# Hybrid RG-LRU, RWKV-7 and mLSTM layer: the state products, the inverse and the scores of two heads as one 128-wide product

## The chip, the cores and the metric

The kernel runs on one core of one Trainium2 chip, alone. The metric is the device time of one launch in microseconds. The kernel before was run three times, and one more execution was profiled; all rows below come from that one.

## What is computed

One layer of a streaming encoder in fp32, on a prompt of 2048 frames and a sample of 32 frames that continues other streams. The cut reference:

```python
hn = rmsnorm(x, norm1)
proj = hn @ w_in                                  # 1024 -> 3072 columns
ya = rmsnorm(rg_lru(causal_conv(pa_x)), norm_a) * gelu(pa_g)      # 256 channels
yb = rwkv7_mix(pb, state)                         # 6 heads x 64
yc = mlstm_mix(pc, state)                         # 6 heads x 64
x = x + concat(ya, yb, yc) @ w_out
gu = rmsnorm(x, norm2) @ w_ffn_in
x = x + (silu(gu[:, :D_FF]) * gu[:, D_FF:]) @ w_ffn_out           # D_FF = 2816
y = rmsnorm(x, norm_f)

# RWKV-7, one frame, per head (64 x 64 state S):
S = S * w_t[None, :] - (S @ kk_t)[:, None] * kka_t[None, :] + v_t[:, None] * k_t[None, :]
y_t = S @ r_t

# mLSTM, one chunk of 64 frames, per head:
scores = (q @ k.T) * exp(log_w - m)
num = w_inter * (q @ C0) + scores @ v
```

All states are outputs too.

## The kernel before

**Layout.** Channels lie on the partitions, frames along the rows. A tile of 128 channels holds two heads of 64, so the six heads of RWKV or mLSTM are three tiles of two, numbered `p` (0 to 2) and `j` (the half, 0 or 1). The prompt is handled in 4 superblocks of 512 frames; the last takes the sample's 32 frames along. The big products (`proj`, tiles `pj` in PSUM) split each fp32 operand into two parts of a shorter format and add three products: `ah,wh`, `al,wh`, `ah,wl`, or `hh`, `hl` for the FFN's hidden values. `phase2` is the output projection, the FFN and the final norm of one superblock. It loads the mixers' outputs from memory (`sq<-ymix`, tile k of 128 channels; k = 0, 1 are RG-LRU, 2 to 4 RWKV, 5 to 7 mLSTM), and `x<-x,pj` evicts into the residual, whose squares `acc` sums for the norm.

**Mixers.** They work in blocks of 128 frames, two chunks of 64, 16 blocks for the prompt and one of 32 frames (one chunk, padded) for the sample: 33 chunks in 17 blocks. `group` records `rwkv`, `mlstm` and `rglru` of one block after another. Their PSUM tiles are called `rw` and `ml`.

RWKV turns the recurrence of a chunk into products. `Fr` holds the scaled keys and receptances of a chunk, with zeros in the other head's half; `SV` holds the state (upper or lower 64 partitions by head) above V. The triangular system of a chunk is inverted in 32x32 blocks: `Hr` goes to memory (`tb`) and back (`xs<-tb`), VectorE does 31 steps of forward substitution (`utmp<-Z,xs`, `Z<-Z,utmp`), Z goes to memory and back (`c<-zb`, the tile `c`, called Zf in the code), and two small products of 32x32 (`ta,Hr` and `c,En`) give the block below the diagonal, where `ta` is the transposed diagonal block (called XT) that VectorE writes. Then per chunk: `xps` = Fr x SV, its copy X1 (tile `zc`), `ups` = Zf x X1, its copy `UV` (with a minus), `sps` = Fr x UV, which is added into the state S; with the state before the chunk, `Un` and `Hr` give the outputs, `hmE` starts their normalisation over the head, `h60E` to `h62E` are its small steps, `yx` is the result, which is transposed by three products with the identity (`cst,yx`), put through E and stored to `ymix`. An fp32 product on TensorE leaves two records in the trace. mLSTM multiplies q and k of a chunk into `sc` (`ml<-q,xi`), weighs the result (`Dm`) into `QS`, and updates its state R.

**Order.** All operations are first recorded with the tiles that they read and write, and `Recorder.order` then lays out every engine's queue by list scheduling, with the planner's own durations (`cost`; an fp32 product that is 64 wide counts 92 ns, one that is 128 wide 217). Mixer operations (priority 1) come ahead of the projections' (2) on TensorE, which fill what is left. A debt counter lets mixer products gather into bursts:

```python
hold = debt > (BURST if burst else 0.0)
...
debt = max(debt, 0.0) + o.dur
...
debt -= o.dur * RATE        # a projection product; RATE = 0.45
```

The queues are then issued in this order; nothing is reordered on the chip. `fill(phase2, ...)` of superblock i is recorded behind the mixers of superblock i, so it fills while the mixers of superblock i + 1 run. The third one, over frames 1024 to 1535, is the last that has mixers beside it; the fourth (544 columns in two pieces of 272) needs all of them.

Of the kernel before, what the change touches and what calls it, by code (L numbers as in the profile page):

```python
# [11 lines left out]
F32 = mybir.dt.float32  # L12
# [32 lines left out]
for _name, _w in (  # L45
    ("ident", 128), ("mar", 128), ("tri", 128), ("blk2", 2), ("mmask", 64), ("smask", 384), ("cmrow", 128),
    ("one", 1), ("sel", 384), ("bones", 128),
):
    CST[_name] = (_n, _w)
    _n += _w  # L50
# [16 lines left out]
def make_consts():  # L67
# [22 lines left out]
    put("smask", np.tile(np.where(t64 == 0, 0.0, 1.0), 6)[None])  # L90
    put("cmrow", np.tile(np.where(t64 == 0, NEG, 0.0), 2)[None])
# [330 lines left out]
def hybrid_kernel(ctx, tc, A, O, cfg):  # L422
# [81 lines left out]
    def setup():  # L504
# [36 lines left out]
        for wn, o in (("wq", 0), ("wk", 36)):  # L541
# [3 lines left out]
            wt = rws.tile([128, 3, 128], F32, tag="c" if o else "ta", name="wt")  # L545
# [269 lines left out]
    def rglru(src, n, st, col):  # L815
        def rt(nm):
            return mls.tile([128, 2, n], F32, tag={"xa": "xi", "r0": "q", "r1": "k", "r2": "Dm", "r3": "WI", "r4": "wl"}[nm], name=nm)
# [84 lines left out]
    def rwkv(src, n_real, nch, st, col):  # L902
# [21 lines left out]
        c_, ta = t3("c"), t3("ta")  # L924
# [20 lines left out]
        V.tensor_tensor_scan(out=cf, data0=C("smask", 0, 3 * n), data1=c_.rearrange("p a t -> p (a t)"), initial=0.0, op0=ALU.mult, op1=ALU.add)  # L945
# [90 lines left out]
        Zf = rw([128, 6, 64], "c")[:, :nq]  # L1036
        for b in range(4):
            h = 32 * (b % 2)
            SY.dma_start(Zf[32 * b:32 * b + 32, :, h:h + 32],
                         zb[:, 32 * nq * b:32 * nq * (b + 1)].rearrange("i (q e) -> i q e", e=32))  # L1040
            if h:
                G.memset(Zf[32 * b:32 * b + 32, :, 0:32], 0.0)
# [24 lines left out]
        V.transpose(out=XT, in_=Zf[:, :, 0:32])  # L1067
# [12 lines left out]
        for q in range(nq):  # L1080
            for j in range(2):
                t, b = slice(64 * j, 64 * j + 32), slice(64 * j + 32, 64 * j + 64)
                PE.matmul(po[t, q, :], NT[b, q, :], Zf[b, q, 32:64], start=True, stop=True,
                          tile_position=(64 * j + 32, 64 * j))
        for j in range(2):
            t = slice(64 * j, 64 * j + 32)
            S.activation(Zf[t, :, 32:64], po[t], AF.Copy, scale=-1.0)
# [550 lines left out]
```

## Time and profile before

| | us |
|---|---|
| three runs | 2846.54, 2850.44, 2855.05 |
| median | 2850.44 |
| profiled execution, own time | 2846.7 |
| its span in the trace | 2844.9 |
| TensorE busy in it | 2749.6 (97%) |
| VectorE busy in it | 2146.1 (75%) |
| mean granted TensorE clock | 0.987 of full speed |

The time contains 1.8 us more than the span from first to last instruction. Busy TensorE time contains matmuls whose ends are modelled and overlap; a product's price is therefore read from the starts of its neighbours. All engine instructions of the kernel share line 332 (the recorder's emit), so the rows are told apart by the tiles' names.

### The profile page before, as it was taken

The numbers are of one execution on the slowest core, as the hardware profiler recorded it, in microseconds if no ns is written. First come the engines' busy times: TensorE is split into PE (matmuls) and PEld (weight loads), VectorE is DVE, ScalarE is ACT, GpSimd is POOL, SyncE is SP. The second block draws the span as 40 slices with busy tenths as digits, with TensorE's granted clock in tenths as the row PEclk, the third lists the DMA queues.
The fourth block names the chain that finished last, engine by engine and source line by source line (L and its number), as shares of the span: only waits on it lengthen the run. The fifth ranks groups of instructions, "written<-read, shape, count | busy, mean of one in ns | idle before, by whom it ended". The sixth has DMA issues, their size and how long they took to land. (4 is left out here: it accounts for less than half of the span.)

```text
span 2844.9 us, 48298 instructions
## 1 busy us (share of the span) xinstructions
PE 2749.6 (97%) x17609; PEld 2310.6 (81%) x17609; DVE 2146.1 (75%) x6009; ACT 1281.1 (45%) x2830; POOL 43.7 (2%) x170
## 2 busy tenths in 40 slices
PE   9999999999999999999999999999999999999998
PEld 7877777889777777777777777777787778999997
DVE  6778877877887878789878888888676676554555
ACT  5555554655553444455444444454433334322223
POOL 0000000000000000000000000000000000000000
PEclk9999999999999999999999999999999999999999
DMA  7453534444323333335233333353332235232232
GB/s 238 133 168 116 179 105 143 138 132 121 121 72 108 88 100 99 95 112 160 73 108 98 89 96 94 100 162 78 100 109 83 84 89 161 81 89 87 88 93 77
DMA packets 235210, 317.92 MB, mean 112 GB/s; under 512 B 63100, under 2 KB 146988, under 8 KB 234844
## 3 DMA queue, kind: packets, MB, share of 16 engines
q1 hardware_dynamic: 233820, 313.72, 37.3%
q8 instruction: 138, 2.26, 0.3%
q10 hardware_dynamic: 1152, 1.11, 0.1%
q14 instruction: 100, 0.82, 0.1%
HBM read 268.50 MB, written 46.27 MB: 111 GB/s over the span
## 5 line engine op out<-in xcount | busy, mean ns | idle before, releaser
L332 PE MATMUL pj<-ah,wh 128*128 128x512 f32 (+1 forms) x2560 | 898.7, 359 | 3.2 <-ACT wh L332 1.1
L332 PE MATMUL pj<-al,wh 128*128 128x512 f32 (+1 forms) x2560 | 898.9, 358 | 2.5 <-DVE al L332 2.5
L332 PE MATMUL pj<-ah,wl 128*128 128x512 f32 (+1 forms) x2560 | 828.8, 356 | 1.5 <-DVE wl L332 1.5
L332 ACT ACTIVATE wh<-raw 128x1024 fp32r<-128x1024 f32 (+2 forms) x444 | 382.3, 861 | 728.8 <-PE pj L332 604.8
L332 PEld LDWEIGHTS pj<-ah,wh 128*128 128x128 f32 x2560 | 484.5, 190 | 68.7 <-ACT ah L332 1.6
L332 PEld LDWEIGHTS pj<-al,wh 128*128 128x128 f32 x2560 | 486.7, 190 | 63.9 <-DVE al L332 3.4
L332 PEld LDWEIGHTS pj<-ah,wl 128*128 128x128 f32 x2560 | 454.9, 189 | 66.8 <-DVE wl L332 3.1
L332 DVE TENSOR_TENSOR wl<-raw,wh 128x1024 fp32r<-128x1024 f32 (+2 forms) x444 | 433.0, 976 | 62.1 <-ACT wh L332 56.4
L332 PE MATMUL pj<-hh,wh 128*128 128x512 f32 (+1 forms) x856 | 299.6, 360 | 9.4 <-ACT hh L332 9.2
L332 PE MATMUL pj<-hl,wh 128*128 128x512 f32 (+1 forms) x856 | 300.9, 359 | 0.1
L332 PE MATMUL pj<-hh,wl 128*128 128x512 f32 (+1 forms) x856 | 280.9, 357 | 0.0
L332 DVE TENSOR_TENSOR x<-x,pj 128x512 f32<-128x512 f32 (+1 forms) x280 | 159.2, 584 | 126.4 <-PE pj L332 122.3
L332 PEld LDWEIGHTS pj<-hh,wh 128*128 128x128 f32 x856 | 160.9, 189 | 35.1 <-ACT hh L332 13.8
L332 PEld LDWEIGHTS pj<-hl,wh 128*128 128x128 f32 x856 | 162.3, 190 | 22.6 <-DVE hl L332 1.7
L332 PE MATMUL pj<-ah,hh 128*128 128x512 f32 (+1 forms) x480 | 170.1, 361 | 6.6 <-ACT hh L332 5.8
L332 PEld LDWEIGHTS pj<-hh,wl 128*128 128x128 f32 x856 | 152.8, 189 | 22.2
L332 PE MATMUL pj<-al,hh 128*128 128x512 f32 (+1 forms) x480 | 169.6, 360 | 0.0
L332 PE MATMUL pj<-ah,hl 128*128 128x512 f32 (+1 forms) x480 | 156.9, 359 | 0.0
L332 DVE TENSOR_TENSOR utmp<-Z,xs 96x60 f32<-96x60 f32 (+27 forms) x527 | 107.0, 203 | 59.1 <-DMA xs<-tb 52.5
L332 DVE TENSOR_TENSOR stg<-stg,pj 128x512 f32<-128x512 f32 (+1 forms) x110 | 62.5, 584 | 91.9 <-PE pj L332 91.3
L332 DVE TENSOR_TENSOR cbuf<-pj,acc 128x512 f32<-128x512 f32 (+1 forms) x110 | 62.7, 586 | 68.9 <-PE pj L332 66.8
L332 DVE TENSOR_TENSOR Z<-Z,utmp 96x60 f32<-96x60 f32 (+27 forms) x527 | 106.6, 202 | 6.4
(344 smaller groups left out, 3835.2 us busy)
## 6 DMA issues: line engine op xcount, KB each, us to landing
raw<-in_w_ffn_in SPq DMA_DIRECT2D x176, 512.0 KB, 3.6
raw<-in_w_ffn_out SPq DMA_DIRECT2D x128, 256.0 KB, 2.7
raw<-in_w_in SPq DMA_DIRECT2D x96, 256.0 KB, 3.1
raw<-in_w_in SPq DMA_DIRECT2D x48, 512.0 KB, 4.1
spill<-stg SPq DMA_DIRECT2D x72, 256.0 KB, 2.9
raw<-in_w_out SPq DMA_DIRECT2D x32, 512.0 KB, 3.5
x<-in_xT SPq DMA_DIRECT2D x48, 256.0 KB, 5.4
raw<-in_w_ffn_out SPq DMA_DIRECT2D x64, 192.0 KB, 2.4
```

The costliest lines, as they stand in the source:

```text
L332: o.fn(*o.args, **o.kw)
```

## The change

In RWKV the two heads of a tile are multiplied as one product. `xps` and `sps` each become 3 products of 128x128 per chunk in place of 6 of 64x64; the two diagonal blocks of the result are read, the off-diagonal ones, across the heads, are left unread. `ups` becomes 3 products of 128x64: for this Zf is widened to 128 columns, the two heads on the diagonal, zeros (GpSimd) elsewhere. The copy X1 is written by two engines, ScalarE the upper and VectorE the lower half; the state add is split by halves; the transpose for `ta` is split by halves.

mLSTM's scores of one block become 6 products of 128x128 in place of 12 of 64x64: both chunks at once, with a persistent tile QM (named `q`), zero outside each head's half; of each product the two blocks of equal chunk are read. To make room, the mLSTM tiles `k` and `mu` go, RG-LRU's `r0` shares a slot ring with `xi`, `r1` takes `KW`, and some constants go.

```diff
@@ rwkv
-        c_, ta = t3("c"), t3("ta")
+        c_, ta = rw([128, 768], "c")[:, :3 * n].rearrange("p (a t) -> p a t", a=3), t3("ta")
...
-        V.tensor_tensor_scan(out=cf, data0=C("smask", 0, 3 * n), data1=c_.rearrange("p a t -> p (a t)"), initial=0.0, op0=ALU.mult, op1=ALU.add)
+        for p in range(3):
+            V.tensor_tensor_scan(out=c_[:, p, :], data0=C("smask", 0, n), data1=c_[:, p, :], initial=0.0, op0=ALU.mult, op1=ALU.add)
...
-        Zf = rw([128, 6, 64], "c")[:, :nq]
+        Zf = rw([128, 6, 128], "c")[:, :nq]
...
+        for j, hs in halves():
+            G.memset(Zf[hs, :, 64 * (1 - j):64 * (1 - j) + 64], 0.0)
...
-        V.transpose(out=XT, in_=Zf[:, :, 0:32])
+        for j in range(2):
+            V.transpose(out=XT[64 * j:64 * j + 32], in_=Zf[64 * j:64 * j + 32, :, 64 * j:64 * j + 32])
...
-            xps = rps("xps")[:, :192].rearrange("p (a t) -> p a t", a=3)
+
+            xps = rps("xps")[:, :384].rearrange("p (a t) -> p a t", a=3)
             for p in range(3):
-                for j, hs in halves():
-                    PE.matmul(xps[hs, p, :], Fr[:, p, c, 0, j, :], SVt[:, p, c, j, :], start=True, stop=True)
+                PE.matmul(xps[:, p, :], Fr[:, p, c, 0, :, :], SVt[:, p, c, :, :], start=True, stop=True)
             X1 = rw([128, 3, 64], "zc")
-            S.activation(X1, xps, AF.Copy)
+            S.activation(X1[0:64], xps[0:64, :, 0:64], AF.Copy)
+            V.tensor_copy(X1[64:128], xps[64:128, :, 64:128])
             ups = rps("ups")[:, :192].rearrange("p (a t) -> p a t", a=3)
             for p in range(3):
-                for j, hs in halves():
-                    PE.matmul(ups[hs, p, :], Z4[hs, p, c, :], X1[hs, p, :], start=True, stop=True)
+                PE.matmul(ups[:, p, :], Z4[:, p, c, :], X1[:, p, :], start=True, stop=True)
...
-            sps = rps("sps")[:, :192].rearrange("p (a t) -> p a t", a=3)
+            sps = rps("sps")[:, :384].rearrange("p (a t) -> p a t", a=3)
             for p in range(3):
-                for j, hs in halves():
-                    PE.matmul(sps[hs, p, :], Fr[:, p, c, 2, j, :], UV[:, p, c, j, :], start=True, stop=True)
-            V.tensor_tensor(out=S0, in0=S0, in1=sps, op=ALU.add)
+                PE.matmul(sps[:, p, :], Fr[:, p, c, 2, :, :], UV[:, p, c, :, :], start=True, stop=True)
+            for j, hs in halves():
+                V.tensor_tensor(out=S0[hs], in0=S0[hs], in1=sps[hs, :, 64 * j:64 * j + 64], op=ALU.add)
...
@@ mlstm
-            S.activation(dst, ps, AF.Copy)
+            if dst is not None:
+                S.activation(dst, ps, AF.Copy)
+            else:
+                for j, hs in halves():
+                    S.activation(QM[hs, :, j, :n], ps[hs], AF.Copy)
...
-        sc = mps("sc")[:, :3 * n].rearrange("p (a c t) -> p a c t", a=3, c=nch)
-        for p in range(3):
+        for j, hs in halves():
+            oh = slice(64, 128) if j == 0 else slice(0, 64)
+            sc = mps("sc")[:, :3 * n].rearrange("p (a t) -> p a t", a=3)
+            for p in range(3):
+                PE.matmul(sc[:n, p, :], k[:, p, :], QM[:, p, j, :n], start=True, stop=True)
             for c in range(nch):
                 cs = slice(64 * c, 64 * c + 64)
-                for j, hs in halves():
-                    oh = slice(64, 128) if j == 0 else slice(0, 64)
-                    PE.matmul(sc[oh, p, c, :], k[hs, p, cs], q[hs, p, cs], start=True, stop=True,
-                              tile_position=(64 * j, 64 * (1 - j)))
-        for j, hs in halves():
-            oh = slice(64, 128) if j == 0 else slice(0, 64)
-            V.tensor_tensor(out=QS[oh, :, :, j, :], in0=sc[oh], in1=ch(Dm)[oh], op=ALU.mult)
-            V.tensor_tensor(out=QS[hs, :, :, j, :], in0=ch(q)[hs], in1=ch(WI)[hs], op=ALU.mult)
+                V.tensor_tensor(out=QS[oh, :, c, j, :], in0=sc[cs, :, cs], in1=ch(Dm)[oh, :, c], op=ALU.mult)
+            V.tensor_tensor(out=QS[hs, :, :, j, :], in0=QM[hs, :, j, :n].rearrange("p a (c t) -> p a c t", c=nch),
+                            in1=ch(WI)[hs], op=ALU.mult)
```

The order of every engine changes too, since the planner's durations and the dependencies differ. Rows of an order show output tile, input tiles and the shape; the numbers behind the names are buffers, and shift by one between the kernels. Three places follow.

TensorE where the third FFN ends, before: the last three output transposes of the sample block (`cst,yx`) stand ahead of the norm sums of the FFN (`cst,acc`), among the first products of the fourth superblock's output projection.

```order
L332 MATMUL pj_202<-ah_0_174,wl_148 128x272
L332 MATMUL pj_202<-ah_0_176,wh_146 128x272
L332 MATMUL pj_202<-al_0_177,wh_146 128x272
L332 MATMUL pj_202<-ah_0_176,wl_148 128x272
L332 MATMUL rw_170<-cst_75,yx_173 128x64 x3
L332 MATMUL pj_203<-cst_75,acc_131 128x1 x4
L332 MATMUL pj_203<-ah_0_174,wh_147 128x272
L332 MATMUL pj_203<-al_0_175,wh_147 128x272
L332 MATMUL pj_203<-ah_0_174,wl_149 128x272
L332 MATMUL pj_203<-ah_0_176,wh_147 128x272
L332 MATMUL pj_203<-al_0_177,wh_147 128x272
L332 MATMUL pj_203<-ah_0_176,wl_149 128x272
```

The same place now: behind the norm sums stand the sample block's small inverse products, and then `xps` (`SV,Fr`) and `ups` (`zc,c`).

```order
L331 MATMUL pj_204<-cst_75,acc_132 128x1 x4
L331 MATMUL rw_171<-ta_172,Hr_130 32x32 x6
L331 MATMUL pj_204<-ah_0_175,wh_148 128x272
L331 MATMUL pj_204<-al_0_176,wh_148 128x272
L331 MATMUL pj_204<-ah_0_175,wl_150 128x272
L331 MATMUL pj_204<-ah_0_177,wh_148 128x272
L331 MATMUL pj_204<-al_0_178,wh_148 128x272
L331 MATMUL rw_170<-c_228,En_231 32x32 x6
L331 MATMUL rw_171<-SV_155,Fr_129 128x128
L331 MATMUL pj_204<-ah_0_177,wl_150 128x272
L331 MATMUL rw_170<-zc_252,c_228 128x64 x2
L331 MATMUL pj_205<-cst_75,rsypj_217 128x128 x4
```

What stood far ahead of this place, under the products of the FFN, now stands in it; the output transposes come 15 rows further down, ahead of the first product of k = 2.

VectorE where the third FFN nears its end, before: the last step of the sample block's inverse (`Z`), and behind it evictions (`stg`, `hl`, `cbuf`) and weight splits (`wl`) of the last FFN group's first half, and the transpose `ta`.

```order
L332 TENSOR_TENSOR Z_245<-Z_245,utmp_246 48x8
L332 TENSOR_TENSOR stg_206<-stg_206,pj_204 128x512
L332 TENSOR_TENSOR stg_206<-stg_206,rb_0_303 128x512
L332 TENSOR_TENSOR wl_149<-raw_145,wh_147 128x1024
L332 TENSOR_TENSOR hl_0_143<-stg_206,hh_0_142 128x512
L332 TENSOR_TENSOR wl_148<-raw_144,wh_146 128x384
L332 TENSOR_TENSOR cbuf_208<-pj_205,acc_130 128x512
L332 TENSOR_TENSOR wl_148<-raw_145,wh_146 128x384
L332 STREAM_TRANSPOSE ta_171<-c_172 128x96
L332 TENSOR_TENSOR al_0_175<-sq_183,ah_0_174 128x544
```

The same steps now: the last step of the inverse stands behind the eviction of `x_4` of the FFN's last output products, the transpose `ta` behind the last of the sums `acc`.

```order
L331 TENSOR_TENSOR utmp_247<-Z_246,xs_227 48x8
L331 TENSOR_TENSOR Z_246<-Z_246,utmp_247 48x8
L331 TENSOR_TENSOR acc_132<-acc_132,cbuf_209 128x512
L331 TENSOR_TENSOR x_5_138<-x_5_138,pj_205 128x512
L331 TENSOR_TENSOR wl_149<-raw_145,wh_147 128x1024
L331 TENSOR_TENSOR x_6_139<-x_6_139,pj_206 128x512
L331 TENSOR_TENSOR acc_132<-acc_132,cbuf_210 128x512
L331 TENSOR_TENSOR x_7_140<-x_7_140,pj_203 128x512
L331 TENSOR_TENSOR acc_132<-acc_132,cbuf_209 128x512
L331 TENSOR_TENSOR wl_150<-raw_146,wh_148 128x1024
L331 TENSOR_TENSOR acc_132<-acc_132,cbuf_210 128x512
L331 STREAM_TRANSPOSE ta_172<-c_228 32x96 x2
```

Both moved towards the end by the whole second half of the last FFN group.

VectorE around the norm of the third FFN, before: the sample block's result (`yx`, then E with the gate `g`) is done ahead of the norm's first small steps (`rsxpj` on); the eight additions to `x` follow the last of these.

```order
L332 TENSOR_TENSOR yx_173<-yx_173,h61E_259 64x384
L332 TENSOR_TENSOR wl_149<-raw_145,wh_147 128x1024
L332 TENSOR_TENSOR acc_131<-acc_131,cbuf_209 128x512
L332 TENSOR_TENSOR E_228<-E_228,bv_241 128x192
L332 TENSOR_TENSOR E_228<-E_228,g_227 128x192
L332 TENSOR_SCALAR rsxpj_213<-pj_203 128x4
L332 TENSOR_SCALAR rsypj_216<-rsxpj_213 128x4
```

Now: the eviction of `UV` comes between the norm's last small step (`rsypj`) and the eight additions, the state's adds and the start of the output normalisation (`hmE`) come behind them.

```order
L331 SCALAR_TENSOR_TENSOR rsypj_217<-rstpj_220,rsypj_217 128x4
L331 TENSOR_SCALAR UV_250<-rw_170 64x3x64
L331 TENSOR_TENSOR x_0_133<-x_0_133,acc_132 128x512
L331 TENSOR_TENSOR x_1_134<-x_1_134,acc_132 128x512
L331 TENSOR_TENSOR x_2_135<-x_2_135,acc_132 128x512
L331 TENSOR_TENSOR x_3_136<-x_3_136,acc_132 128x512
L331 TENSOR_TENSOR x_4_137<-x_4_137,acc_132 128x512
L331 TENSOR_TENSOR x_5_138<-x_5_138,acc_132 128x512
L331 TENSOR_TENSOR x_6_139<-x_6_139,acc_132 128x512
L331 TENSOR_TENSOR x_7_140<-x_7_140,acc_132 128x512
L331 TENSOR_TENSOR S_0_221<-S_0_221,rw_171 64x192 x2
L331 TENSOR_REDUCE hmE_254<-rw_170 64x6
```

The sample block's last part moved behind the eight additions, which before came after all of it.

## Rows read from the trace of the kernel before

**Rows 1.** The page: its span and the busy time of each engine.
```profile
span 2844.9 us, 48298 instructions
...
PE 2749.6 (97%) x17609; PEld 2310.6 (81%) x17609; DVE 2146.1 (75%) x6009; ACT 1281.1 (45%) x2830; POOL 43.7 (2%) x170
```

**Rows 2.** TensorE by instruction and shape: count, busy us, mean ns, idle before.
```profile
L332 PE MATMUL rw<-SV,Fr 128*64 128x64 f32 x792 | 60.1, 227 | 0.0
```

**Rows 3.** TensorE's timeline, a lone 64-wide batch: start us, duration us, instruction, count.
```profile
1326.96 0.40 PE L332 MATMUL pj<-ah,wh 128*128 128x512 f32 x1
1327.19 0.40 PE L332 MATMUL pj<-al,wh 128*128 128x512 f32 x1
1327.52 0.57 PE L332 MATMUL rw<-UV,Fr 128*64 128x64 f32 x12
...
1328.36 0.39 PE L332 MATMUL pj<-ah,wh 128*128 128x512 f32 x1
```

**Rows 4.** TensorE's timeline, a lone 128-wide batch.
```profile
125.61 0.39 PE L332 MATMUL pj<-al,hh 128*128 128x512 f32 x1
125.84 0.87 PE L332 MATMUL rw<-Fr,BK 128*128 128x128 f32 x6
...
126.78 0.40 PE L332 MATMUL pj<-ah,hh 128*128 128x512 f32 x1
```

**Rows 5.** TensorE's timeline, batches that stand together.
```profile
115.60 1.50 PE L332 MATMUL rw<-Fr,BK 128*128 128x128 f32 x12
116.86 0.48 PE L332 MATMUL pj<-ah,wh 128*128 128x512 f32 x1
...
204.31 0.57 PE L332 MATMUL rw<-UV,Fr 128*64 128x64 f32 x12
204.81 0.68 PE L332 MATMUL ml<-R,KW 64*64 64x65 f32 x16
205.43 0.50 PE L332 MATMUL pj<-ah,wh 128*128 128x512 f32 x1
```

**Rows 6.** VectorE's waits; TensorE's timeline at one; window of all engines around it.
```profile
DVE utmp L332 <- DMA xs<-tb: 52.5, 17, 6.3
...
1111.53 0.59 PE L332 MATMUL ml<-cst,WI 128*128 128x1 f32 x2 [3.61 <-DVE WI L332]
...
1109.00:1119.00 10.00, 7.47 (x26) 6.30 (x27) 8.17 (x33) 5.65 (x12) 0.00 (x0) 0.66 0.30 86
```

**Rows 7.** TensorE's timeline at the end of the fill; window, projection products alone.
```profile
2363.35 0.39 PE L332 MATMUL pj<-hh,wl 128*128 128x512 f32 x1
2363.58 0.29 PE L332 MATMUL pj<-ah,wh 128*128 128x272 f32 x1
2363.71 0.28 PE L332 MATMUL pj<-al,wh 128*128 128x272 f32 x1
...
2366.72 1.05 PE L332 MATMUL pj<-cst,acc 128*128 128x1 f32 x8 [0.85 <-DVE acc L332]
...
2373.64 1.27 PE L332 MATMUL pj<-ah,wh 128*128 128x272 f32 x4
...
2363.60:2390.00 26.40, 19.69 (x109) 17.51 (x108) 1.63 (x4) 0.60 (x1) 0.74 0.79 264
```

**Rows 8.** TensorE's and VectorE's timeline, the sample block's RWKV chain.
```profile
2339.69 0.38 PE L332 MATMUL rw<-ta,Hr 32*32 32x32 f32 x12
...
2344.18 0.36 DVE L332 TENSOR_SCALAR UV<-rw 64x192 f32<-64x192 f32 x1
...
2350.30 0.55 DVE L332 TENSOR_REDUCE hmE<-rw 64x6 f32<-64x384 f32 x1 [0.58 <-PE rw L332]
...
2358.66 0.16 DVE L332 TENSOR_TENSOR h62E<-h61E 64x6 f32<-64x6 f32 x1
...
2364.39 0.54 DVE L332 TENSOR_TENSOR yx<-yx,h61E 64x384 f32<-64x384 f32 x1
...
2371.79 4.91 DVE L332 TENSOR_TENSOR x<-x,acc 128x512 f32<-128x512 f32 x8 [1.84 <-ACT acc L332]
```

More of the change, by code (lines that the diff above doesn't have):

```diff
@@ L45 @@
 for _name, _w in (
-    ("ident", 128), ("mar", 128), ("tri", 128), ("blk2", 2), ("mmask", 64), ("smask", 384), ("cmrow", 128),
+    ("ident", 128), ("mar", 128), ("tri", 128), ("blk2", 2), ("mmask", 64), ("smask", 128),
     ("one", 1), ("sel", 384), ("bones", 128),
@@ L89, in make_consts @@
     put("mmask", np.where(s[:, None] <= t64[None], 0.0, NEG))
-    put("smask", np.tile(np.where(t64 == 0, 0.0, 1.0), 6)[None])
-    put("cmrow", np.tile(np.where(t64 == 0, NEG, 0.0), 2)[None])
+    put("smask", np.tile(np.where(t64 == 0, 0.0, 1.0), 2)[None])
     put("one", 1.0)
@@ L544, in setup @@
                 PE.transpose(pt[:, p, :], W(wn, 128 * p, 128 * p + 128), ident)
-            wt = rws.tile([128, 3, 128], F32, tag="c" if o else "ta", name="wt")
+            wt = rws.tile([128, 3, 128], F32, tag="kr" if o else "ta", name="wt")
             S.activation(wt, pt, AF.Copy)
@@ L816, in rt @@
         def rt(nm):
-            return mls.tile([128, 2, n], F32, tag={"xa": "xi", "r0": "q", "r1": "k", "r2": "Dm", "r3": "WI", "r4": "wl"}[nm], name=nm)
+            if nm in ("xa", "r0"):
+                return mls.tile([128, 4, n], F32, tag="xi", name=nm)[:, 0:2, :] if nm == "xa" else mls.tile([128, 4, n], F32, tag="xi", name=nm)[:, 2:4, :]
+            return mls.tile([128, 2, n], F32, tag={"r1": "KW", "r2": "Dm", "r3": "WI", "r4": "wl"}[nm], name=nm)
         xa = rt("xa")
@@ L1082, in rwkv @@
                 t, b = slice(64 * j, 64 * j + 32), slice(64 * j + 32, 64 * j + 64)
-                PE.matmul(po[t, q, :], NT[b, q, :], Zf[b, q, 32:64], start=True, stop=True,
+                PE.matmul(po[t, q, :], NT[b, q, :], Zf[b, q, 64 * j + 32:64 * j + 64], start=True, stop=True,
                           tile_position=(64 * j + 32, 64 * j))
@@ L1086, in rwkv @@
             t = slice(64 * j, 64 * j + 32)
-            S.activation(Zf[t, :, 32:64], po[t], AF.Copy, scale=-1.0)
+            S.activation(Zf[t, :, 64 * j + 32:64 * j + 64], po[t], AF.Copy, scale=-1.0)
         py = rw([128, 6, 64], "yx")
@@ L1204, in ch @@
             return x.rearrange("p a (c t) -> p a c t", c=nch)
-        q = t3("q")
-        k = t3("k") if st else xa
-        for w_, dst in (((W("wq").rearrange("p (a e) -> p a e", a=3), q), (W("wk").rearrange("p (a e) -> p a e", a=3), k))
-                        if st else ((wqk, q),)):
+        k = t3("KW") if st else xa
+        for w_, dst in (((W("wq").rearrange("p (a e) -> p a e", a=3), None), (W("wk").rearrange("p (a e) -> p a e", a=3), k))
+                        if st else ((wqk, None),)):
             ps = mps("qk")[:, :3 * n].rearrange("p (a t) -> p a t", a=3)
@@ L1239, in mlstm @@
         PE.transpose(rp[0:72, 0:n], WIDE[1][:n], ident[:n, :n])
-        mu = ml([6, 128], "mu")[:, :n]
-        V.tensor_tensor_scan(out=mu, data0=C("cmrow", 0, n)[0:6], data1=rp[0:6, 0:n], initial=NEG,
-                             op0=ALU.add, op1=ALU.max)
+        RW = RWW[0:6]
+        mu = RW[:, 0:n]
+        mu3 = mu.rearrange("p (c t) -> p c t", c=nch)
+        for c in range(nch):
+            V.tensor_tensor_scan(out=mu3[:, c, :], data0=bc(C("smask", 0, 1)[0:6], [6, 64]), data1=rp[0:6, 64 * c:64 * c + 64],
+                                 initial=NEG, op0=ALU.add, op1=ALU.max)
         R, mr = ml_state[st]
-        mu3 = mu.rearrange("p (c t) -> p c t", c=nch)
         tl = ml([6, 2], "tl")[:, :nch]
@@ L1249, in mlstm @@
         V.tensor_tensor_scan(out=mr[:, 1:1 + nch], data0=bl, data1=tl, initial=mr[:, 0:1], op0=ALU.add, op1=ALU.max)
-        RW = RWW[0:6]
         V.tensor_copy(RW[:, n:n + nch], mr[:, 0:nch])
         V.tensor_tensor(out=mu3, in0=mu3, in1=bc(mr[:, 0:nch, None], [6, nch, 64]), op=ALU.max)
-        V.tensor_scalar(out=RW[:, 0:n], in0=mu, scalar1=-1.0, scalar2=None, op0=ALU.mult)
+        V.tensor_scalar(out=mu, in0=mu, scalar1=-1.0, scalar2=None, op0=ALU.mult)
         mr2 = ml([6, 4], "mr", bufs=2)
@@ L1489, in hybrid_kernel @@
     RWW = mls.tile([128, 130], F32, name="RWW")
-    for u in (LZ, *WIDE, RWW):
+    QM = mls.tile([128, 3, 2, 128], F32, name="q")
+    for u in (LZ, QM, *WIDE, RWW):
         G.memset(u, 0.0)
```

5 lines of the change are left out of this document (3 added, 2 removed).

## The prediction, made before the changed kernel was run

> **What bounds the kernel now.** I read the busy shares first: TensorE is busy 97% of the span and VectorE about three quarters [rows 1]. So the sum of TensorE work sets the time, and only three things can move it: the cost of the mixers' products between the projection products that fill TensorE, the places where TensorE stands still, and the half clock that follows them. Next the groups of TensorE instructions: the products that the change touches carry short names of their own, `rw<-SV,Fr`, `rw<-UV,Fr`, `rw<-zc,c` and `ml<-q,xi`, and an fp32 product leaves two records, as 33 chunks x 12 products x 2 = 792 shows [rows 2]. The mean of such a record (227 ns) is its length in the pipeline and no price, since records overlap; prices are read from a timeline, as the distance between the starts of fill products on both sides of a batch. Last I looked at where TensorE waits: it is not where these products lie, but behind VectorE, when that sits on `utmp<-Z,xs` until the DMA `xs<-tb` lands, and at the end of the fill.
>
> **Prices of the products.** Fill products of 512 columns follow each other at 0.23 us (1326.96 to 1327.19). A lone batch of six 64-wide products (12 records) lies between fill products that start at 1327.19 and 1328.36, with one more fill product between them: 1.17 us less two pitches is about 0.70 [rows 3]. A lone batch of three 128-wide products (6 records) takes 125.61 to 126.78, again 1.17 and 0.70 [rows 4]. So one RWKV batch, halved in number and doubled in width, costs the same when it stands alone. To price batches that stand together I need the record and the switch apart. Two neighbouring 64-wide batches start 0.50 us (12 records) and 0.62 us (16 records) before what follows them, so four records more cost 0.12: 0.030 each. Twelve 128-wide records start 1.26 us before the next fill: 0.105 each; the lone batch gives at most 0.70/6 = 0.117; I take 0.111 [rows 5]. The 64-wide lone batch is then 0.36 of records and 0.34 for going to 64-wide and back, 0.17 a switch, and if an eviction shadow is in it as in the 128-wide one (0.70 against 0.63 for six records at 0.105) 0.145; I take 0.16.
>
> The order of TensorE loses 786 products of the narrow kind (198 each for `xps`, `ups`, `sps`, 192 scores) and gains 393 wide ones. That is 786 records at 0.111 = +87.2, 1572 records at 0.030 = -47.2. The places where neighbouring products differ in tile size fall from 644 to 367: 277 x 0.16 = -44.3. Sum **-4 us**. With 0.117 and 0.145 it is +4.6, with 0.105 and 0.17 it is -11.8.
>
> The Trainium skill, "TensorEngine Tiling (Array Packing)", Key Properties, says that changing the tiling mode drains TensorE. The trace agrees in sign: lone 64-wide batches pay about 0.34 us more than their records cost.
>
> **VectorE and ScalarE.** Per chunk VectorE gets the copy of the lower half of X1 and a second add into the state, each of the 64x192 form that took 0.36 [rows 8]: 33 x 0.72 = 24 us; scans in pieces, scores' products in four pieces instead of two, and the transpose in two bring, by the same sort of piece, an estimated 12 more. ScalarE's extra pieces and GpSimd's 34 memsets lie on engines under half busy. The 36 us are 1.7% of VectorE's 2146 [rows 1]. If none of them is on the path they cost 0; if TensorE's whole 95 us without work (span less busy) stretched in proportion, 1.6; twice that and more where a stretch is already late, 4. I take **+1.5**.
>
> **The end of the fill.** This is the largest term. Before, the last product of the third FFN, the last fill there is, starts at 2363.35, and at 2363.58 the output projection of the last 544 columns begins with k = 0 and 1, whose inputs are ready (24 products of 272 columns). By then the sample block has only its output transposes left on TensorE; the norm sums of the FFN follow at 2366.72, and the product of k = 2, which needs RWKV's output, starts at 2373.64 [rows 7]. Between 2363.58 and 2390.00 there are 109 records, of which 97 are such products (8 are `acc`, 4 `rsypj`) [rows 7]: at the 0.125 of their undisturbed pitch (2363.58 to 2363.71 is one) 12.1 of 26.4 us. So this stretch loses 14.3 us today.
>
> In the order of the changed kernel the sample block is later by a whole chain. VectorE's last step of the inverse, which before stood ahead of five evictions that still belong to the fill, now stands behind the eviction of `x_4` of the last FFN group, and the transpose of the inverse behind the last `acc`. On TensorE `rw<-ta,Hr` comes after `pj<-cst,acc`, that is after the fill has ended. What ran from 2339.69 to 2364.93 under cover of fill [rows 8] now runs with almost none. Counted from 2363.58:
> - The norm sums come at +3.1 as today (2366.72), and `ta`, `c,En`, `xps`, `ups` go one after another in and behind them. Before, `rw<-ta,Hr` to the eviction of the outputs `hmE` took 10.6 (2339.69 to 2350.30) with fill between.
> - VectorE then has the eight `x<-x,acc` between the eviction of UV and the state's add and `hmE`. Before they lay at +8.2 to +13.1 (2371.79 plus 4.91) [rows 8]; now the copy of X1 and the eviction of UV stand inside and behind the small norm steps ahead of them. I add 1.5 for these: +14.6. Since ta at +4 plus 10.6 is also +14.6, the two agree.
> - The state's two adds, 0.7: `hmE` at +15.3. From there to the end of `yx` it was 14.6 before (2350.30 to 2364.93), between fill evictions; its own work is 0.55 + 0.16 + 0.54, ScalarE's square of about 0.5, one more reduction of 0.54, some ten tiny steps like `h62E` (0.16, about 0.2 with the start) and the last multiplication of 0.54 [rows 8], with the handovers about 5.5: +20.8.
> - From the end of `yx` to the product of k = 2 (transposes, the store to `ymix`, the load of `sq`, the split) it was 2364.93 to 2373.64, 8.7: **+29.5**.
>
> The stretch loses 29.5 less 24 x 0.125 = 26.5, and 3.4 of half clock behind the gap (half of the 6.8 us below). What it no longer costs is today's 14.3, and six batches of RWKV (ta, En, xps, ups, sps, outputs) of about 0.70 that lay between fill products and now lie in the gap, 4.2. 26.5 + 3.4 - 14.3 - 4.2 = **+11.4**. If `hmE` to `yx` ran at ScalarE's and VectorE's bare durations and the x additions hardly moved, it would be +5; if the 14.6 stayed half as it was, +17.
>
> **The sum.** -4 + 1.5 + 11.4 = +8.9 on the profiled execution's 2846.7: 2855.6. That execution is 3.7 below the median of the three runs, so **2859.3** beside 2850.4.
>
> **Half clock.** At 1111.53 TensorE had waited 3.61 us behind VectorE, and the 10 us around it have a granted clock of 0.66, a mean of the two levels 2.4 and 1.2 GHz: 6.8 us stood at the lower one [rows 6]. If all of these were worked through, 3.4 is lost, if the wait is one part of them, 1.6; between them 2.6. One such wait is worth 3.6 + 2.6 = 6.2 us. VectorE met 17 waits for `xs<-tb`, 52.5 us [rows 6], of which only a few reach TensorE.
>
> **The rivals.** (0.3% of this kernel is 8.6 us, and its three runs differ by as much; less than that a measurement can hardly tell from no change.)
> - A, as summed, 0.44: 2853 to 2866.
> - B, the gap at the end is mostly covered, 0.16. For it: the x additions could be ready sooner, since the norm's small steps cost only 0.2 each; against it: their place in VectorE's order ahead of `hmE`. End +5: 2852.9.
> - E, the batches stand together more often than my two lone batches show, and the products come out at -11.8, 0.14: 2851.5. For it: `xps` stands right behind the 32-wide `c,En` products in both orders. Against: the lone batches cost equal.
> - C, not slower, 0.12: the shifted order puts VectorE on `xs<-tb` a little later, and two of the long waits that now reach TensorE vanish, -12.4: 2846.9. One is enough to fall to the middle of no change (2853.1); with two the whole is below before. For it: VectorE has 1.7% more to do before each such wait, and so arrives later; against it: what it does is itself late.
> - D, two such waits more, 0.11: 2871.7.
> - F, the saved switches cost nothing, since what the narrow products lose by them they regain by running side by side, 0.03: then only +87.2 - 47.2 = +40 of records stand in place of the -4, 44 above A: 2903. Against it: lone batches would then differ by 0.3, and they are equal [rows 3, 4].
>
> The Trainium skill, "TensorEngine Tiling (Array Packing)", Key Properties and Theoretical Speedup, has tiles work in parallel, up to twice as fast where one dimension is at most 64, which speaks against the change. The record price of 0.030 for a 64-wide one against 0.111 for a 128-wide one bears that out for batches that stand together, and the lone batches show it eaten up by the switches.
>
> The range takes in C at one end and D at the other: 2846 to 2873, with F and the tails outside. Faster by over 0.3% needs C with B or E: 0.08. A lies across the upper bound of no change (2859.0), so B, E, most of C and somewhat under half of A are the same, 0.47; the rest of A, D and F are slower, 0.45.
>
> **What would show it.** Right: in the changed profile TensorE's idle time before `rw<-cst,yx` or `pj<-ah,wh` near the end of the third FFN rises by over 8 us, the last `rw<-ta,Hr` lies behind the last `pj<-hh,wl` of that FFN, `hmE` behind the eight `x<-x,acc`, and a lone `rw<-UV,Fr` of six records still takes about 0.7. Wrong: the product of k = 2 starts under +20 after the fill's end (B), the mixers' batches take under 0.6 (E), or the waits for `xs<-tb` that reach TensorE change by more than one (C, D).

## The result and the profile after

The changed kernel takes 2886.98 us in the median of four runs (2885.24 to 2893.62) against 2850.23 for four of the kernel before: ratio 1.0132, 95% interval 1.0109 to 1.0155, so 36.8 us slower. The forecast was 2859.3, and its range ended at 2873. The profiled execution took 2885.3 us. The page of the changed kernel, span and busy time of each engine, answers to [rows 1]:

```profile
span 2883.3 us, 46942 instructions
...
PE 2758.9 (96%) x16823; PEld 2348.2 (81%) x16823; DVE 2179.5 (76%) x6174; ACT 1294.0 (45%) x2847; POOL 58.0 (2%) x205
```

TensorE has 786 records fewer, as counted, and 9 us more busy time; the span is 38 us longer, so most of the loss, 29 us, is time in which TensorE stands idle. VectorE has 33 us more work (estimated: 36).

Where it is lost shows when the span is cut at the end of the fill, the last product of the third FFN. "The fill" is from here on the stretch from the first projection product to this one. The windows of all engines before and after it, first of the kernel before, then of the changed kernel (length, then PE, PEld, DVE, ACT and POOL busy, the granted clock, DMA share, GB/s; the second window begins with the last fill product and reaches to the start of the 101st product of 272 columns behind it):

```profile
5.82:2363.35 2357.53, 2289.47 (x14008) 1854.37 (x14009) 1887.87 (x5448) 1130.21 (x2573) 39.36 (x144) 0.99 0.39 115
2363.35:2390.55 27.20, 20.82 (x118) 18.52 (x116) 16.84 (x37) 10.26 (x17) 0.00 (x0) 0.75 0.77 258
```

```profile
5.98:2390.43 2384.45, 2296.05 (x13167) 1888.58 (x13167) 1914.94 (x5591) 1139.67 (x2580) 53.02 (x178) 0.99 0.37 113
2390.43:2431.19 40.76, 24.02 (x173) 22.31 (x172) 23.67 (x60) 13.81 (x27) 0.00 (x0) 0.75 0.54 178
```

The stretch behind the fill went from 27.2 to 40.8 us (+13.6), the fill from 2357.5 to 2384.5 (+26.9). Inside the fill, length less PE busy is the time in which TensorE stands: 68.1 before, 88.4 now (+20.3). The clock records of the two traces show the lower level (1.2 GHz) for 40.5 us of TensorE's working time in the fill before, and 53.9 now. One such stretch of the changed kernel, at a granted clock of 0.50 behind a wait of 3.22 us:

```profile
867.12 0.79 PE L331 MATMUL pj<-hl,wh 128*128 128x512 f32 x1 [3.22 <-DVE hl L331]
867.71 0.63 PE L331 MATMUL pj<-hh,wl 128*128 128x512 f32 x1
868.14 0.63 PE L331 MATMUL pj<-hl,wh 128*128 128x512 f32 x1
```

Fill products follow each other at 0.43 us here in place of 0.23, so nearly half of the time at the lower level is lost. Counted as half, that is 20.3 and 26.9 (+6.7). What is left of the fill, TensorE's work at full clock, is the same to 0.1 us in both kernels. But products of the sample block that lay inside the fill before, where their batches took 4.5 us, now lie behind its end; so by this count the products cost about 4.5 us more.

The end, TensorE's timeline of the changed kernel, answers to [rows 7]:

```profile
2390.43 0.40 PE L331 MATMUL pj<-hh,wl 128*128 128x512 f32 x1
2390.66 0.29 PE L331 MATMUL pj<-ah,wh 128*128 128x272 f32 x1
...
2393.95 1.05 PE L331 MATMUL pj<-cst,acc 128*128 128x1 f32 x8 [1.33 <-DVE acc L331]
2394.93 0.38 PE L331 MATMUL rw<-ta,Hr 32*32 32x32 f32 x12
...
2402.32 1.19 PE L331 MATMUL rw<-UV,Fr 128*128 128x128 f32 x6
...
2404.62 0.39 PE L331 MATMUL rw<-SV,Fr 128*64 128x64 f32 x4
2412.10 0.58 PE L331 MATMUL rw<-cst,yx 64*128 64x64 f32 x3 [7.09 <-DVE yx L331]
2419.95 1.27 PE L331 MATMUL pj<-ah,wh 128*128 128x272 f32 x4 [7.26 <-ACT ah L331]
```

and VectorE's, which answers to [rows 8]:

```profile
2393.81 0.58 DVE L331 STREAM_TRANSPOSE ta<-c 32x96 f32<-32x96 f32 x2
...
2400.47 0.36 DVE L331 TENSOR_SCALAR UV<-rw 64x192 f32<-64x192 f32 x1 [2.01 <-PE rw L331]
2400.86 4.91 DVE L331 TENSOR_TENSOR x<-x,acc 128x512 f32<-128x512 f32 x8
...
2406.55 0.55 DVE L331 TENSOR_REDUCE hmE<-rw 64x6 f32<-64x384 f32 x1
...
2411.49 0.55 DVE L331 TENSOR_TENSOR yx<-yx,h61E 64x384 f32<-64x384 f32 x1
```

The fill ends at 2390.66, and the product of k = 2 starts at 2419.95: +29.3, where +29.5 was forecast. `hmE` stands behind the eight `x<-x,acc`, at +15.9 (forecast +15.3); `yx` ends at 2412.04, +21.4 (forecast +20.8). The two waits of 7.09 and 7.26 us are the gap: first for the output normalisation on VectorE, then for the store to `ymix` and its load.

The waits in the fill are of another kind than I had looked for. Waits over 1.7 us are 12 where they were 11 (37.0 against 33.7 us); those of 0.25 to 1.7 us went from 51 to 83 and from 31.0 to 46.7 us. Of these short ones VectorE ended 50 (31 before) and ScalarE 31 (20 before), and 70 stand ahead of a mixer's product (40 before). Some of TensorE's waits by what ended them, over the whole span (us in total, times, longest), of the kernel before:

```profile
PE ml L332 <- DVE WI L332: 8.7, 4, 3.6
...
PE ml L332 <- DVE R L332: 4.1, 5, 2.1
PE ml L332 <- DVE QS L332: 4.0, 6, 1.3
PE rw L332 <- DVE ta L332: 3.8, 4, 1.6
...
PE ml L332 <- DMA xi<-spill: 3.1, 1, 3.1
```

Now of the changed kernel, where the row on `yx` holds the gap, and where one row, on `WI`, fell:

```profile
PE ml L331 <- DVE R L331: 10.8, 10, 3.1
PE ml L331 <- DMA xi<-spill: 9.6, 4, 5.4
...
PE rw L331 <- DVE yx L331: 7.8, 3, 7.1
...
PE ml L331 <- DVE QS L331: 6.8, 10, 2.0
...
PE rw L331 <- DVE ta L331: 5.3, 10, 1.3
...
PE ml L331 <- DVE WI L331: 2.0, 1, 2.0
```

VectorE's waits for the inverse's transfer are nearly those of [rows 6] (52.5 us in 17):

```profile
DVE utmp L331 <- DMA xs<-tb: 54.4, 17, 6.8
```

### The profile page after: what moved, and what is told of

Its sections match the earlier page's. It is cut to its first block, busy times and chain, and to the rows that moved or that the text cites. A ratio compares the mean times of both kernels' runs of the same rounds, so it can differ in the third digit from the quotient of the medians.

```text
span 2883.3 us, 46942 instructions
## 1 busy us (share of the span) xinstructions
PE 2758.9 (96%) x16823; PEld 2348.2 (81%) x16823; DVE 2179.5 (76%) x6174; ACT 1294.0 (45%) x2847; POOL 58.0 (2%) x205
## 3 DMA queue, kind: packets, MB, share of 16 engines
q1 hardware_dynamic: 233820, 313.53, 35.6%
## 5 line engine op out<-in xcount | busy, mean ns | idle before, releaser
L331 PEld LDWEIGHTS pj<-ah,wh 128*128 128x128 f32 x2560 | 484.3, 189 | 73.8 <-ACT ah L331 7.5
```

Source lines behind the costliest of these rows:

```text
L331: o.fn(*o.args, **o.kw)
```

## The experiments

Of every run three numbers are read from its trace in the way above: the waits in the fill (length less PE busy, plus half of the working time at the lower clock), the mixers' batches (the distance between the fill products on both sides of each batch, less two pitches and less the waits in it, halved where the clock is the lower one, all added), and the stretch from the end of the fill to the 101st product behind it. Each kernel was profiled once and timed in 4 to 12 runs; the time is the median against that of the kernel before on the same chip, and no run reaches 2% either way.

The differences of the three numbers from the kernel before add up to the difference of the two profiled executions within 5 us in every row, so less than that is not read from them. Most profiled executions lie within 4 us of their kernel's median. Below it by more are unshare_s36 (10.6 us), narrow_dve (9.6), after_s44 (7.0), score_unshare (6.8) and after_s36 (5.5); their waits are those of an execution that falls short of the median by as much. That of the kernel before lies 3.7 below.

| run | median, us | ratio (interval) | waits in the fill | batches | behind the fill |
|---|---|---|---|---|---|
| before | | | 88.3 | 484.4 | 27.2 |
| changed kernel | +36.8 | 1.0132 (1.0109 to 1.0155) | 115.3 | 486.1 | 40.8 |
| rwkv_only | +32.5 | 1.0109 (1.0090 to 1.0128) | 86.2 | 503.6 | 52.3 |
| score_only | +9.8 | 1.0032 (1.0019 to 1.0046) | 117.1 | 457.6 | 42.3 |
| narrow_dve | +12.4 | 1.0035 (1.0019 to 1.0050) | 88.2 | 480.7 | 41.0 |
| unshare | +17.3 | 1.0059 (1.0046 to 1.0072) | 99.2 | 487.3 | 42.5 |
| before_s36 | +14.9 | 1.0059 (1.0038 to 1.0080) | 97.9 | 479.2 | 43.1 |
| before_r48 | +5.7 | 1.0020 (1.0009 to 1.0032) | 100.5 | 486.8 | 22.8 |
| after_r48 | +31.9 | 1.0114 (1.0097 to 1.0131) | 122.0 | 487.5 | 23.8 |
| unshare_r48 | +15.9 | 1.0054 (1.0038 to 1.0070) | 113.5 | 484.3 | 21.9 |
| before_share | +28.7 | 1.0097 (1.0084 to 1.0110) | 116.7 | 475.9 | 46.7 |
| after_s36 | +33.4 | 1.0116 (1.0098 to 1.0133) | 110.8 | 485.9 | 40.9 |
| unshare_s36 | +33.1 | 1.0104 (1.0087 to 1.0121) | 108.2 | 483.5 | 41.0 |
| after_s44 | +9.5 | 1.0034 (1.0020 to 1.0048) | 81.5 | 485.6 | 42.6 |
| unshare_s44 | +29.3 | 1.0102 (1.0085 to 1.0119) | 104.9 | 486.9 | 41.0 |
| score_only_s44 | +23.1 | 1.0083 (1.0069 to 1.0097) | 116.9 | 464.3 | 50.0 |
| score_unshare_s44 | +9.1 | 1.0027 (1.0015 to 1.0039) | 104.6 | 471.0 | 40.6 |
| score_unshare | -10.3 | 0.9958 (0.9942 to 0.9974) | 92.8 | 467.7 | 26.1 |
| score_unshare_s36 | -5.6 | 0.9987 (0.9975 to 0.9999) | 99.5 | 472.4 | 25.4 |
| score_unshare_r46 | -7.6 | 0.9977 (0.9961 to 0.9993) | 97.2 | 472.2 | 25.1 |

Three theories stand behind the expectations. Theory 1 was that the end of the fill costs 9 to 15 us whatever the products are, and that the waits inside come from two additions: RG-LRU's gate tile in xi's slot, which holds back the load of the next block, and VectorE's pieces. Its rivals: theory 2, the wide products cost TensorE more; theory 3, any new order draws new waits.

### The parts of the change

rwkv_only is RWKV's half of the diff, with the scan of the running maximum by chunks; score_only is mLSTM's and RG-LRU's half. narrow_dve is the kernel before with VectorE's pieces alone:

```diff
-            S.activation(X1, xps, AF.Copy)
+            S.activation(X1[0:64], xps[0:64], AF.Copy)
+            V.tensor_copy(X1[64:128], xps[64:128])
...
-            V.tensor_tensor(out=S0, in0=S0, in1=sps, op=ALU.add)
+            for j, hs in halves():
+                V.tensor_tensor(out=S0[hs], in0=S0[hs], in1=sps[hs], op=ALU.add)
```

> RWKV's products, inverse and evictions as in the changed kernel (and its scan of the running maximum by chunks), mLSTM's scores and tiles as before, RG-LRU's tiles not shared with xi. In the order the sample block's last part still stands behind the end of the fill, so every theory expects the gap there, +9 us. Theory 1 (the waits inside the fill come from the pieces added on VectorE and from RG-LRU sharing xi's slot): VectorE's pieces of RWKV alone give about half of the 24 us that went missing inside the fill, so +18 to +25 us in all, and waits of TensorE for the DMA xi<-spill fall back from 9.6 to about 3 us. Theory 2 (wide products cost TensorE more than the narrow ones): three quarters of the products are here, so +25 to +30 us. Theory 3 (any new order draws new waits): between 0 and +40, without relation to the parts.

> mLSTM's scores, tile QM, maximum scan and RG-LRU's shared slot as in the changed kernel, RWKV as before. The sample block's last part stands behind the end of the fill here too: +9 us. Theory 1: the shared slot (waits for xi<-spill of 9 to 10 us against 3.1) and QS in four pieces bring the other half of the 24 us: +18 to +25 us. Theory 2: a quarter of the products, +12 to +16 us. Theory 3: no relation to the parts.

> The kernel before with all its narrow products, but X1 copied by ScalarE and VectorE in halves and the state added in halves, as in the changed kernel: only VectorE's load and the hand-overs change. The order puts the sample block's last part behind the end of the fill here too, so +9 us are expected whatever the products cost. Theory 1: VectorE's 24 us of added pieces bring 6 to 12 us of waits more: +15 to +21. Theory 2: nothing beyond the gap, +9 to +11. Theory 3: between 0 and +25.

In time, rwkv_only lies above what theories 1 and 2 gave it, score_only below both, and narrow_dve between them; neither theory holds by the times alone.

The batches tell the products apart. RWKV's wide ones cost 19 us more than the narrow ones, the scores save 27 (12 to 27 over the six kernels with wide scores alone, against the one order of the kernel before; its own three orders lie between 479.2 and 486.8). Five pairs that differ in RWKV's half alone, with the same slot and the same planner constants, agree: the changed kernel has 28.5 us more of batches than score_only, unshare 20 more than score_unshare, and the pairs at SLACK 44 and 36 below have 11 to 21 more.

narrow_dve has the waits of the kernel before (88.2 and 88.3) with the added VectorE pieces in, and what it loses lies behind the fill. As its profiled execution lies 9.6 us below its median, the medians are a second reading: 12.4 us less the 13.8 behind the fill, plus the 3.7 that its batches are shorter, leaves 2. So the pieces cost little under the fill, but no cost is shown only to within some 6 us. rwkv_only loses more behind the fill (25 us) than by its products: in its order the last steps of the inverse, too, stand behind the end, and TensorE waits 3.4 us for `ta` there.

Why the two halves differ is seen on single batches. `sps` with the outputs behind it, TensorE's timeline before and after:

```profile
1471.33 0.40 PE L332 MATMUL pj<-ah,wl 128*128 128x512 f32 x1
1471.66 0.57 PE L332 MATMUL rw<-UV,Fr 128*64 128x64 f32 x12
...
1473.39 0.39 PE L332 MATMUL pj<-al,wh 128*128 128x512 f32 x1
```

```profile
1367.10 0.40 PE L331 MATMUL pj<-ah,wh 128*128 128x512 f32 x1
1367.34 0.83 PE L331 MATMUL rw<-UV,Fr 128*128 128x128 f32 x6
...
1369.36 0.40 PE L331 MATMUL pj<-ah,wl 128*128 128x512 f32 x1
```

Before, from fill start to fill start 2.06 us with 24 records, now 2.26 with 16, although two of the outputs' records now stand elsewhere. Batches of this make-up occur 14 times in either trace, nearly all at these lengths to 0.01 us. The narrow `sps` shared its tile size with the output products behind it, and the wide one adds its records without taking a switch away. At 33 chunks, 0.20 us each are 7 of the 19 us; where the rest lies is not shown. A piece of the scores, before and after:

```profile
927.72 0.40 PE L332 MATMUL pj<-ah,wh 128*128 128x512 f32 x1
928.04 0.44 PE L332 MATMUL ml<-q,xi 64*64 64x64 f32 x4
...
928.76 0.39 PE L332 MATMUL pj<-ah,wl 128*128 128x512 f32 x1
```

```profile
882.24 0.40 PE L331 MATMUL pj<-hh,wh 128*128 128x512 f32 x1
882.48 0.38 PE L331 MATMUL ml<-q,xi 128*128 128x128 f32 x2
...
882.94 0.39 PE L331 MATMUL pj<-hh,wl 128*128 128x512 f32 x1
```

Two narrow products, alone between fill products, take 1.04 us from fill start to fill start, which less two pitches is 0.57; the wide one that replaces them takes 0.70, which leaves 0.23. In the planner's bursts the scores come in such pieces, and each paid two switches where it stood alone. The Trainium skill, "TensorEngine Tiling (Array Packing)", Key Properties, names the drain at a change of mode; these rows agree. The prediction's own prices give the same signs: neighbours of unequal tile size are 644 before, 525 with RWKV wide and 468 with the scores wide, thus 65.9 - 35.6 - 19.0 = +11 for RWKV (wide records, narrow records, switches) and 21.3 - 11.5 - 28.2 = -18 for the scores.

### The slot of RG-LRU's gate tile

```diff
-            if nm in ("xa", "r0"):
-                return mls.tile([128, 4, n], F32, tag="xi", name=nm)[:, 0:2, :] if nm == "xa" else mls.tile([128, 4, n], F32, tag="xi", name=nm)[:, 2:4, :]
-            return mls.tile([128, 2, n], F32, tag={"r1": "KW", "r2": "Dm", "r3": "WI", "r4": "wl"}[nm], name=nm)
+            return mls.tile([128, 2, n], F32, tag={"xa": "xi", "r0": "QS", "r1": "KW", "r2": "Dm", "r3": "WI", "r4": "wl"}[nm], name=nm)
```

The edit is unshare's. before_share is the reverse: the kernel before with `r0` in `xi`'s slot.

> The changed kernel, with RG-LRU's gate tile (r0, gb) in the slot of QS in place of xi's. If the shared slot makes the load of the next block's xi late (theory 1), TensorE's waits for xi<-spill fall from 9.6 to about 3 us, some half clock goes with them, and the time falls by 8 to 10 us against the changed kernel, to +27 to +29 over before. Theory 2: no change against the changed kernel, +36 to +39. The end of the fill is unchanged in the order, so the +9 stays.

> The kernel before with RG-LRU's gate tile r0 moved into xi's slot (the sharing alone, no product changed). The order puts the sample block's transposes 3.0 us of fill behind the end, so +13 to +16 for the gap, as in before with SLACK 36, which came out at +15. If the sharing costs 20 us of waits and half clock inside the fill: +30 to +38. If not: +13 to +18.

The mechanism is there. Idle time of the engines before instructions on `xi`, until its load landed (us, times), in the changed kernel and in unshare:

```profile
  DMA xi<-spill: 42.4, 24
```

```profile
  DMA xi<-spill: 17.4, 11
```

Unshare's median is 19 us below the changed kernel's, where 8 to 10 were expected. In the two traces its fill is 15.9 us shorter: 10.8 are TensorE's standing (88.4 to 77.6), 5.4 the clock. To see whether that is the slot or the order that came with it, pairs were run in other orders: SLACK, a margin of the planner, at 36 or 44 in place of 40.

```diff
-SLACK = 40.0
+SLACK = 36.0
```

> The changed kernel with SLACK 36: another order of the same work, the sample block behind the end of the fill as in the changed kernel. If sharing the slot costs about 20 us: +33 to +40 again. If the +37 of the changed kernel came from one unlucky order: +15 to +25.

> The same order constant (SLACK 36) with RG-LRU's gate tile in the slot of QS. If sharing costs about 20 us whatever the order: 15 to 22 us below the run with the slot shared and SLACK 36, near +17. If the difference found at SLACK 40 was luck of the order: within 6 us of the shared one.

> The changed kernel with SLACK 44, the sample block 3.0 us of fill behind the end. If the slot costs 15 to 20 us in most orders: +30 to +38. If the +37 and +33 of its two sisters were the order: anything from +12.

> The same with RG-LRU's gate tile in the slot of QS. If the slot costs 15 to 20 us in most orders: that much below the run with the slot shared. If SLACK 36, where the pair was equal, is the rule: within 6 us of it.

> Wide scores alone, with the shared slot, SLACK 44: the scores save about 18 us, the end of the fill costs 14, the slot 15 to 20: +8 to +18. Without a cost of the slot: -6 to +2.

> Wide scores alone, RG-LRU's gate tile in the slot of QS, SLACK 44. Its sample block ends behind the fill, so it has the gap of 14 us that its sister at SLACK 40 (-10) had not: 0 to +8, and 15 to 20 us below the run with the slot shared if that costs in most orders; equal to it if not.

Of six pairs that differ in the slot, the shared one is slower by 20 (wide scores alone, SLACK 40: score_only against score_unshare below), 19 (SLACK 40), 16 (RATE 0.48) and 14 us (wide scores alone, SLACK 44), equal at SLACK 36, and faster by 20 us at SLACK 44. In the first pair 16 us of the stretch behind the fill are in the difference, as only one of the two ends in time. before_share makes no clean pair: it is 14 us slower than before_s36, which ends as far behind the fill in its order but differs in SLACK too. Its +28.7 lies between its own two expectations. The mean of the six, 8, is well inside their spread: a steady cost of 15 to 20 is not shown, and theory 1 falls in that part.

What the slot costs TensorE directly can be read from the traces. Its waits for `xi<-spill`, shared and not, are 9.6 and 3.6 us at SLACK 40, 9.6 and 3.9 at SLACK 36, 3.6 and 4.3 at SLACK 44, 10.3 and 4.2 at RATE 0.48, and with wide scores alone 7.6 and 3.4, then 7.6 and 5.9 at SLACK 44. So the slot adds 2 to 6 us there in five of the six pairs and nothing in the sixth; what it costs by way of the other engines is not separated from the order. Four of these runs lie outside all that was expected of them: after_s44 below, unshare_s44, score_only_s44 and score_unshare_s44 above. What stands is theory 3, scatter: the same work in four orders (changed kernel at SLACK 36, 40, 44 and RATE 0.48) has 110.8, 115.3, 81.5 and 122.0 us of waits in its fill, with batches within 2 us. The fill and the stretch behind it of after_s44, and three of its waits:

```profile
6.56:2355.01 2348.45, 2283.50 (x13167) 1880.11 (x13168) 1913.31 (x5591) 1139.28 (x2580) 53.20 (x178) 0.99 0.38 115
2355.01:2397.58 42.57, 26.17 (x174) 24.17 (x172) 23.72 (x60) 13.76 (x27) 0.00 (x0) 0.68 0.51 171
```

```profile
PE rw L331 <- DVE yx L331: 6.7, 2, 6.5
...
PE ml L331 <- DVE R L331: 4.4, 7, 1.2
PE ml L331 <- DMA xi<-spill: 3.6, 1, 3.6
```

Its fill is 36 us shorter than the changed kernel's and 9 shorter than that of the kernel before, in an execution 7 us below its median; by the medians it is 27 us faster than the changed kernel.

### The end of the fill

> The kernel before with one planner constant changed (SLACK 36 in place of 40): every product and eviction as before, only the order differs, and in it the sample block's last part stands behind the end of the fill, with its output transposes 3.0 us of fill behind it. Theory 1 (the place of that chain costs 13 to 15 us, whatever the products are): +10 to +16 us. Theory 2 (wide products or added VectorE work cost the time): no change, within 4 us of before.

The kernel before, one planner constant changed: every product is narrow, yet the sample block comes behind the end. TensorE's timeline there:

```profile
2372.88 0.38 PE L332 MATMUL rw<-ta,Hr 32*32 32x32 f32 x12 [0.87 <-DVE rsxpj L332]
...
2389.94 0.58 PE L332 MATMUL rw<-cst,yx 64*128 64x64 f32 x3 [7.91 <-DVE yx L332]
2398.41 1.27 PE L332 MATMUL pj<-ah,wh 128*128 128x272 f32 x4 [7.89 <-ACT ah L332]
```

The fill ends at 2367.67, and the product of k = 2 starts 30.7 us later, where the changed kernel has 29.3. The stretch behind the fill is 15.9 us longer than before, and the time +15, inside theory 1's +10 to +16; the 9.6 us of waits that this order adds in the fill are more than half made up by shorter batches.

```diff
-RATE = 0.45
+RATE = 0.48
```

> The changed kernel with RATE 0.48 in place of 0.45, so that mixer products get more of TensorE and the sample block's transposes stand 14 us of fill ahead of its end, none of its chain behind. Theory 1: the gap at the end goes, 13 to 15 us less than the changed kernel, and if what remains is the shared slot it is +15 to +23 over before. Theory 2: the products are the same, so the time stays at +33 to +37.

> RG-LRU's gate tile in the slot of QS, and RATE 0.48: the sample block ends 32 us of fill ahead of the end. Theory 1: both named causes are gone, 13 to 15 us below the run with the slot alone changed: 0 to +5 over before. Theory 2: still +17 over before.

> The kernel before with RATE 0.48, the control for the two others: its sample block ends 50 us of fill ahead of the end. Before, it just ended in time, with a loss of about 14 us in the stretch behind the fill, of which some 5 to 10 can go when the outputs lie ready: -10 to -3 us by theory 1. Theory 2 has no reason for a change: within 4 us.

RATE 0.48 brings the mixers forward. The stretch behind the fill falls to 22 to 24 us in all three, below the 27.2 of before, so the gap is the place of that chain and not the products. The time hardly follows, and all three miss what theory 1 gave them (+15 to +23, 0 to +5, -10 to -3): the fill gets 13 to 16 us longer against the same kernels at 0.45. Of that 7 to 14 are waits; in the changed kernel about half is work, with the chain's products back in the fill. The gain is given back there.

### A version that beats both

Wide scores, RWKV as before, the gate tile in the slot of QS. In its order the sample block ends as it did before.

> mLSTM's scores as 128-wide products with the tile QM, RG-LRU's gate tile in the slot of QS (no sharing with xi), RWKV as before. In the order the sample block ends as it did before (its transposes 1.5 us of fill behind the end, as before), so no gap is added. By the profiles so far the wide scores save TensorE 23 to 27 us between the fill products, while the shared slot costs about 20 us of waits and half clock: this kernel should keep the first without the second, -15 to -25 us. If the sharing is not what the waits come from (they come with any new order), +0 to -10.

```profile
6.06:2355.31 2349.25, 2275.27 (x13817) 1850.67 (x13818) 1886.29 (x5496) 1143.19 (x2590) 39.26 (x144) 0.99 0.39 115
2355.31:2381.36 26.05, 20.85 (x118) 18.44 (x116) 16.83 (x37) 10.25 (x17) 0.00 (x0) 0.74 0.77 269
```

Two more orders of it end in time too:

> Wide scores alone, RG-LRU's gate tile in the slot of QS, SLACK 36; the sample block ends in time (0.8 us of fill behind the end). By the three terms: scores -18, end 0, waits inside the fill +0 to +25 against before, as the order falls: -18 to +7. The stretch behind the fill takes 26 to 28 us, the mixers' batches 455 to 472.

> The same with SLACK 40 and RATE 0.46, ending in time too (1.5 us of fill behind the end): again -18 to +7, with 26 to 28 us behind the fill and batches of 455 to 472.

All three are faster than the kernel before, by 0.1 to 0.4%, the second one only just clear of no change. Their batches are 12 to 17 us below, the stretch behind the fill 1 to 2 below, waits 4 to 11 above. All three end in time; score_unshare_s44, the same kernel in an order that does not, is slower than the kernel before by 9.1 us. The first, at -10, missed the -15 to -25 that a steady cost of the slot would have given.

## Why the prediction was wrong

- **The products**, -4 forecast, with bounds of -11.8 and +4.6: 486.1 against 484.4 us of batches, +2. But in the changed kernel the sample block's batches, 4.5 us, have left the fill. Between kernels with the chain in the same place it is +7 (the changed kernel against before_s36) and +1 (both at RATE 0.48). So the term came out near its upper bound, 5 to 11 us above its value; that is about what the batches scatter from order to order. I did not price the two halves of the change apart, although the switches were counted from the orders. They pull against each other.
- **VectorE**, +1.5 forecast, with 33 of the expected 36 us more work: 0 by narrow_dve's profile and +2 by its median, neither of them sharp.
- **The end of the fill**, +11.4 forecast: that was +15.6 for the stretch behind the fill less 4.2 for the six batches that leave the fill. Measured are +13.6 and 4.5, which makes +9.1; the term is right to some 2 us, and each step of the chain to 0.7 us. That it belongs to the order and not to the products is shown by before_s36, which pays it with the old products, and by after_r48, which has the new ones and does not.
- **Waits inside the fill**: the step that failed. The sum has no term for them. I let the 88 us of waits and half clock of the kernel before stand, and gave them only the rivals C and D, of two long waits more or less at 6.2 us each, with 0.11 for the side that came true; even that side had the wrong kind of wait. They rose by 27, some 70% of the profiled execution's loss of 38.6. Long waits hardly changed in number; thirty-two more short ones came, 15.7 us, behind VectorE and ScalarE in many places, and with them 6.7 us more of half clock. New orders of one kernel redraw them: from 81.5 to 122.0 in four orders of the changed kernel (mean 107), 88.3 to 100.5 in three of the kernel before (mean 96). The order of before lies at the low end of its own and near the low end of all twenty, so a reordering had more to lose than to gain, and a scatter of some 40 us, had it been known, would have set the range.

Open is which feature of an order makes its waits: neither the shared slot nor VectorE's load tells the good from the bad ones by itself. Open is also whether the change raises them beyond the draw of an order, since the two means are closer than the orders of either kernel.

## What to carry to other kernels

When a planner lays out the queues, a change of any part is also a new order: read how far the waits scatter over a few harmless values of a planner constant before a difference of one per cent is put down to the change. Here widening small products paid where they stood in pieces among products of another tile size, and cost time where their neighbours shared the size; price each group with its neighbours, not alone. And look at what is last under the cover of the fill: here a chain of 25 us that slipped past its end cost 14 with narrow products and with wide ones.

## What the runs showed that I had not expected

The same instructions on all engines, in an order that differs by one planner margin, differ by 27 us in the median (after_s44 against the changed kernel, +9.5 and +36.8), with some 2 us of difference in TensorE's work. Between runs of one kernel the time moves by up to 23 us (the kernel before, 2836.66 to 2860.01 in 23 runs on one chip), so a single profile stands for a kernel's waits only within some 10 us. And 0.1 to 0.4% was to be had by taking the scores' half of the change and leaving RWKV as it was.
